# Two-layer hybrid denoiser: the first right operands made in two goes, and the last four readouts of a layer given places of their own and split where they stand

## The chip, the core and the metric

The kernel runs on one core of one Trainium2 chip. The core has TensorE (PE in the profile), which multiplies matrices from SBUF into PSUM; VectorE (DVE), ScalarE (ACT) and GpSimd (POOL), which work element by element; and SyncE (SP), which issues all of this kernel's DMA transfers, one behind the other. Each engine takes its instructions in a fixed order and waits on semaphores for what another engine, or a transfer, has to deliver first. The metric is the device time of one execution in microseconds; lower is better.

## The reference, cut to what matters

Two layers work on 512 latent columns and 256 context columns of width 1024. Each layer has a feed-forward block, a mixing stage and a second feed-forward block, and each of the three is fed with a normalised input that is scaled and shifted by values computed from a condition vector:

```
mx  = split(silu(c) @ w_mod[l] + b_mod[l], 9)        # shift, scale, gate of each of the 3 blocks
x  += 0.5 * mx[2] * swiglu(rms_norm(x)*(1+mx[1]) + mx[0], ffn_up, ffn_down)
...
p   = nx @ w_in[l]                                   # mixing
attn_x = neighbourhood_attention(q, k, v, ...)       # 4 head pairs
o   = o_fwd + o_bwd                                  # RWKV scans in both directions
o   = (o - mean(o)) * rsqrt(var(o) + eps) * lnx_gain + lnx_bias
rwkv_x = (o + bonus) * g                             # the readout
y_x = concat(attn_x, rwkv_x) @ w_out[l]              # the output projection
x  += mx[5] * y_x
```

The second feed-forward block has the form of the first. In the last layer the context is needed only as far as it feeds the latent part.

## The kernel before

All data are kept with features on the 128 partitions and the 768 columns (latent, then context) along the free axis. A product in near-float32 is made of three matmuls: each operand is split into a high part (ACT rounds it) and a low part (DVE subtracts the high part from the original), `split`, L208; lines L171 and L165 in the profile are the helpers that issue an ACT activation and an elementwise two-operand operation.

**Feed-forward blocks.** The up projection is a Strassen-Winograd product: features and columns are halved, and seven products replace eight. Its seven right operands are made from sums and differences of four quarters of the scaled input, and its left ones from those of the weights (`raw`; POOL makes s and rewrites raw). `prep_wino` (L258) makes the right operands of one of four feature tiles, with the tile four further on: it scales both (`xs0`, `xs1`) on ACT with the modulation's scale `gs`, appends two columns each of the modulation's shift (`mods[l][:, 3*s]`) for latent and context at the ends of the halves, so that the shift goes through the product as columns of its own, and makes seven high/low pairs (`part`; the tile name is `b`). Three differences are POOL's, one is DVE's. Each half has `XH` = 386 columns, of which the last four carry the shift. The root mean square is applied behind the product, so the operands do not need it. `prep_begin` (L216) asks for the first weights (`up_weights`) and hands out the places of the operands.

At the start `run` (L1119) makes modulation 1 (the scale; a layer has nine such, each from `mod`, L174: matmuls over weight tiles, here four of 2048 columns, a copy `modsb` on DVE, two transpositions, and the addition of the bias, `mods`, on DVE), loads x, makes modulation 0 (the shift) to its end, and then calls `prep_begin` and `prep_wino` four times. The first seven products of the up projection (PSUM tile `mw`, L369; their combination on DVE is `up_g<-up_g,mw`) follow.

**Mixing.** Six generators run at once: the RWKV chains, their solves, their blocks, the projections, the attention and the output projection, with the later modulations as another filler. `drive` (L81) gives them priorities, chains first; at the build a scheduler deals the instructions of each engine from these into one fixed order. RWKV's eight heads are two groups; a group's chain (`rwkv_chain`, L919) goes through six pieces of 128 tokens in both directions. When it has both directions of a piece, a readout follows (`rwkv_read`, L992): piece 0 and 1 are context, 3, 4, 2, 5 latent, and the chain's last two pieces release two readouts each, 3 and 4, then 2 and 5. A readout is

- `pj` (PE, the backward output turned over), `o` = forward + `pj` (DVE), mean and its subtraction (DVE, POOL, POOL), square (ACT), sum, root, reciprocal, product (DVE, ACT, DVE, POOL; the small results are `rst`);
- `pt` (two transpositions on PE), each scaled on ACT into `ry`; `ry` + `bv`, the bonus (POOL);
- `pg` (two matmuls on PE: the gate), `ry` times `pg` (DVE), and a store of both halves into `yd` in DRAM.

Its five SBUF tiles come from the pool `ro`, which has five places, thus one readout's worth; `pj`, `pt` and `pg` share the two PSUM banks of `a`. Other pools: `st`, eight places of 2048 columns; `x`, `r`, `g3`, `z`.

The output projection goes in four pairs of feature tiles: two of the attention (k = 0 to 3), that of RWKV's group 0 (k = 4, 5), and last that of group 1 (k = 6, 7). For each pair `mix_out` (L1032) loads both tiles from `yd` (`yl`, 128x768, or 128x512 in layer 1), splits them whole into `o2`, and runs 8 output tiles (`accumulate`, L428: `mm`, L327). Behind each output tile of the last pair `to_ffn` makes the operands of the second feed-forward block with `prep_wino`, whose first weights (`raw`) are asked for there.

Of the kernel before, what the change touches and what calls it, by code (L numbers as in the profile page):

```python
# [109 lines left out]
class Net:  # L110
# [147 lines left out]
    def prep_wino(self, kt, tag="g3"):  # L258

        l, s = self.prep_key  # L260
        h = self.half(self.prep_ctx)
        x0, x1 = [self.t(tag, f"xs{i}", 2 * XH) for i in range(2)]
        for k, t in ((kt, x0), (kt + 4, x1)):
            for xs, j in ((LAT, 0), (CTX, 1))[:2 if self.prep_ctx else 1]:
                self.act(t[:, xs], self.x[k][:, xs], AF.Copy, scale=self.gs[l, s][:, k, j:j + 1])
            self.act(t[:, 2 * h - 4:2 * h].rearrange("p (a c) -> p a c", a=2), free_ap(self.mods[l][:, 3 * s, k], [[0, 2], [1, 2]]), AF.Copy)
# [8 lines left out]
        part(1, x1[:, a])  # L275
        self.tt(x0[:, a], x0[:, b], x0[:, a], ALU.subtract, self.nc.gpsimd)
# [9 lines left out]
        self.squares(kt + 4)  # L286

# [631 lines left out]
    def rwkv_chain(self, l, i, last):  # L919
# [8 lines left out]
        for u in range(6):  # L928
            emit = not (last and u < 2)
            yield from self.until(lambda: g["applied"] > u)  # L930
            bl = lambda y, e, d, c: self.block(g["stage"][y, u], e, d, c)
# [28 lines left out]
            self.chained[i] = u + 1  # L960
            for b in ((), () if last else (0, 1), (), (), (3, 4), (2, 5))[u]:
# [29 lines left out]

    def rwkv_read(self, l, i, u, of, ob):  # L992
# [3 lines left out]
        bv = self.t("ro", "bv").rearrange("p (y t) -> p y t", y=2)  # L996
        for y in range(2):
            nc.sync.dma_start(out=bv[:, y], in_=self.bvd[2 * i + y][:, sl])
# [3 lines left out]
        o = self.t("ro", "o").rearrange("p (y e v) -> p y e v", y=2, e=2)  # L1002
# [6 lines left out]
        sq = self.t("ro", "osq").rearrange("p (n v) -> p n v", n=4)  # L1009
# [6 lines left out]
        yt = self.t("ro", "ry").rearrange("p (y t) -> p y t", y=2)  # L1016
# [4 lines left out]
        gg = self.t("ro", "gg")  # L1021
        nc.sync.dma_start(out=gg, in_=self.a["gg2"][l][:, 256 * i:256 * i + 256])
# [4 lines left out]
        n = NL + 128 * u if u < 2 else 128 * u - NC  # L1027
        for y in range(2):
# [3 lines left out]
    def mix_out(self, l, ctx, k0, n, tag, after):  # L1032
# [3 lines left out]
        for k in range(k0, k0 + n):  # L1036
            t = self.t("z", "yl", T)
            self.nc.sync.dma_start(out=t[:, 0:w], in_=self.yd[k][:, 0:w])
# [80 lines left out]
    def run(self, out):  # L1119
# [7 lines left out]
        for _ in self.mod(0, 0, "st", SW, "g"):  # L1127
            pass
# [132 lines left out]
```

## Time and profile before

| | us |
|---|---|
| median of 3 runs | 3911.8 (3909.35 to 3918.2) |
| profiled execution, its own time | 3917.2 |
| its span | 3915.4 |
| PE busy | 3616.3 (92%) |
| DVE busy | 2924.9 (75%) |
| ACT busy | 1496.0 (38%) |
| POOL busy | 1013.9 (26%) |

The profiled execution is 5.4 us above the median, and 1.8 us of it lie outside its span. The page divides the span into 40 slices of 97.9 us; a digit is the busy share of an engine in tenths, and the row PEclk is the clock granted to PE in tenths of full speed. A timeline row has the start in us from the span's start, the duration in us, the engine, the line, and the operation with its tiles, output first. SPq is a transfer that SP has issued. A view by stretch gives each engine's busy microseconds between two times, a view by lines groups equal instructions with their mean in ns.

### The profile page before, as it was taken

The numbers are of one execution on the slowest core, as the hardware profiler recorded it, in microseconds if no ns is written. First come the engines' busy times: TensorE is split into PE (matmuls) and PEld (weight loads), VectorE is DVE, ScalarE is ACT, GpSimd is POOL, SyncE is SP. The second block draws the span as 40 slices with busy tenths as digits, with TensorE's granted clock in tenths as the row PEclk, the third lists the DMA queues.
The fourth block names the chain that finished last, engine by engine and source line by source line (L and its number), as shares of the span: only waits on it lengthen the run. The fifth ranks groups of instructions, "written<-read, shape, count | busy, mean of one in ns | idle before, by whom it ended". The sixth has DMA issues, their size and how long they took to land. (4 is left out here: it accounts for less than half of the span.)

```text
span 3915.4 us, 73285 instructions
## 1 busy us (share of the span) xinstructions
PE 3616.3 (92%) x28980; PEld 3121.2 (80%) x28980; DVE 2924.9 (75%) x5618; ACT 1496.0 (38%) x2968; POOL 1013.9 (26%) x1156
## 2 busy tenths in 40 slices
PE   6999999999798898799999999999998996879999
PEld 4789998787565666699998999998786665768999
DVE  5678786666777765888788887886668677668988
ACT  4233334334343432533335333334434343234433
POOL 2222230202222211322224222230203223123443
PEclk7999999999797889899999999999998896788999
DMA  5421112322354243111121111113332431121222
GB/s 196 124 88 65 68 63 100 102 91 75 96 155 129 83 149 118 64 65 65 68 84 47 62 65 68 65 65 118 101 103 82 149 112 48 61 91 65 84 101 86
DMA packets 216535, 354.60 MB, mean 91 GB/s; under 512 B 46720, under 2 KB 131072, under 8 KB 203904
## 3 DMA queue, kind: packets, MB, share of 16 engines
q1 hardware_dynamic: 216192, 349.91, 27.4%
q8 instruction: 229, 3.75, 0.4%
q14 instruction: 114, 0.93, 0.1%
HBM read 306.31 MB, written 43.52 MB: 89 GB/s over the span
## 5 line engine op out<-in xcount | busy, mean ns | idle before, releaser
L369 PE MATMUL mw<-b,wq 128*128 128x386 f32 (+1 forms) x4224 | 787.0, 329 | 19.4 <-DVE wq L165 15.1
L369 PEld LDWEIGHTS mw<-b,wq 128*128 128x128 f32 x4224 | 704.0, 191 | 39.3 <-DVE wq L165 19.3
L327 PE MATMUL mm<-h,whi 128*128 128x256 f32 (+1 forms) x2816 | 652.6, 326 | 2.6 <-ACT h L171 0.8
L369 PE MATMUL mw<-b,whi 128*128 128x386 f32 (+1 forms) x2112 | 518.4, 328 | 24.6 <-DVE b L165 11.3
L327 PEld LDWEIGHTS mm<-h,whi 128*128 128x128 f32 x2816 | 467.6, 188 | 59.6 <-issue 8.5
L168 DVE SCALAR_TENSOR_TENSOR x<-mm,mods,x 128x256 f32<-128x256 f32 (+1 forms) x704 | 390.7, 581 | 159.5 <-PE mm L327 157.1
L327 PE MATMUL mm<-h,wlo 128*128 128x256 f32 (+1 forms) x1408 | 440.6, 325 | 2.7 <-DVE wlo L165 2.3
L369 PEld LDWEIGHTS mw<-b,whi 128*128 128x128 f32 x2112 | 374.1, 191 | 32.2 <-DVE b L165 14.0
L171 ACT ACTIVATE whi<-wraw 128x512 fp32r<-128x512 f32 x312 | 195.8, 629 | 500.2 <-PE mm L327 298.3
L165 DVE TENSOR_TENSOR wq<-raw,wq 128x512 fp32r<-128x512 f32 x352 | 313.2, 892 | 52.0 <-ACT wq L171 50.1
L369 PE MATMUL mw<-b,wlo 128*128 128x386 f32 (+1 forms) x1056 | 347.0, 329 | 3.4 <-DVE wlo L165 3.0
L171 ACT ACTIVATE wq<-raw 128x512 fp32r<-128x512 f32 x352 | 220.1, 629 | 312.1 <-PE mw L369 288.8
L327 PEld LDWEIGHTS mm<-h,wlo 128*128 128x128 f32 x1408 | 261.8, 188 | 29.5 <-DVE wlo L165 4.4
L165 DVE TENSOR_TENSOR wlo<-wraw,whi 128x512 fp32r<-128x512 f32 x312 | 224.9, 723 | 57.7 <-ACT whi L171 34.3
L165 DVE TENSOR_TENSOR up_g<-up_g,mw 128x386 f32<-128x386 f32 (+1 forms) x352 | 182.0, 518 | 86.1 <-PE mw L369 77.1
L165 POOL TENSOR_TENSOR raw<-raw,s 128x512 f32<-128x512 f32 x88 | 123.8, 1407 | 407.3 <-DVE wq L165 404.8
L165 POOL TENSOR_TENSOR s<-raw 128x512 f32<-128x512 f32 x88 | 125.2, 1423 | 394.8 <-DVE wlo L165 317.3
L171 ACT ACTIVATE whi<-s 128x512 fp32r<-128x512 f32 x176 | 110.0, 628 | 281.9 <-PE mm L327 198.9
L165 POOL TENSOR_TENSOR up_g<-up_g,rstd 128x386 f32<-128x386 f32 (+1 forms) x88 | 107.5, 1221 | 405.1 <-DVE up_g L165 405.1
L327 PE MATMUL mm<-x,whi 128*128 128x258 f32 (+2 forms) x832 | 208.5, 337 | 0.0
L369 PEld LDWEIGHTS mw<-b,wlo 128*128 128x128 f32 x1056 | 201.2, 191 | 7.4 <-DVE wlo L165 6.5
L188 PE MATMUL modps<-wmod,cs 128*32 128x256 f32 x1152 | 168.7, 441 | 30.7 <-DMA wmod<-in_w_mod_dram 30.0
(226 smaller groups left out, 7009.8 us busy)
## 6 DMA issues: line engine op xcount, KB each, us to landing
raw<-in_ffn_up_dram SPq DMA_DIRECT2D x88, 1024.0 KB, 5.2
wmod<-in_w_mod_dram SPq DMA_DIRECT2D x208, 256.0 KB, 3.0
wraw<-in_ffn_down_dram SPq DMA_DIRECT2D x176, 256.0 KB, 3.1
wraw<-in_w_in_dram SPq DMA_DIRECT2D x104, 256.0 KB, 2.8
wmod<-in_w_mod_dram SPq DMA_DIRECT2D x96, 128.0 KB, 2.3
wmod<-in_w_mod_dram SPq DMA_DIRECT2D x8, 1024.0 KB, 10.6
wraw<-in_w_out_dram SPq DMA_DIRECT2D x32, 256.0 KB, 3.2
in<-rkv SPq DMA_DIRECT2D x20, 384.0 KB, 4.2
```

What stands on the lines that cost most here:

```text
L165: (eng or self.nc.vector).tensor_tensor(out=out, in0=a, in1=b, op=op)
L168: self.nc.vector.scalar_tensor_tensor(out=out, in0=a, scalar=s, in1=b, op0=op0, op1=op1)
L171: self.nc.scalar.activation(out, in_, f, **kw)
L188: nc.tensor.matmul(ps[q:q + 32], lhsT=self.cs[:, kt], rhs=w, start=kt == 0, stop=kt == KD - 1)
L327: nc.tensor.matmul(ps, lhsT=wt, rhs=xt[k][:, c0:c1], start=k == 0 and n == 0, stop=k == nk - 1 and n == 2)
L369: nc.tensor.matmul(ps, lhsT=wt[:, c], rhs=self.bs[i][k][xt], start=k == 0 and m == 0, stop=k == 3 and m == 2)
```

## The change

**Right operands in two goes.** `run` now calls `prep_begin` ahead of modulation 0 and takes one step of that modulation behind each `prep_wino`. These four calls have `shifts=False`: operands 0 and 1 are made on all 386 columns, as before, but on what stands in the last four then; operands 2 to 6 on 382. What the last four columns will need of `xs0` and `xs1` POOL copies into a small tile `edge`. When the shift is there, `prep_shifts` makes the four differences of these columns for all tiles at once (DVE, 128x16) and splits them into the operands' last columns, 20 splits of 128x4.

**A layer's end.** In the last group (i = 1), when the chain comes to its fifth piece, four tiles of `st` are taken, one for each of the readouts 3, 4, 2 and 5 (name `read`, all five parts of a readout in it), and the bonus and the gate's weights are loaded into them at once (`read_begin`). Behind the fifth piece `last_inputs` takes two more, `o2`, the operands of the last pair; in layer 0 it fills their context columns from `yd`. The four readouts (`direct`) then split their product `yt` straight into the columns of `o2`, and `mix_out` takes `o2` for the last pair without a load. The diff, cut to its core:

```diff
@@ prep_wino @@
+            if shifts:
+                self.act(t[:, 2 * h - 4:2 * h]..., free_ap(self.mods[l][:, 3 * s, k], ...), AF.Copy)
...
-            self.split(src, hi, lo)
+            w = src.shape[-1]
+            self.split(src, hi[:, 0:w], lo[:, 0:w])
...
         part(1, x1[:, a])
+        if not shifts:
+            for i, t in enumerate((x0, x1)):
+                self.nc.gpsimd.tensor_copy(self.edge[:, i, kt], t[:, n:h])
+            a, b = slice(0, n), slice(h, h + n)
...
+    def prep_shifts(self):
...
+        self.tt(c[4], s0, e0, ALU.subtract)
+        self.tt(c[3], s1, s0, ALU.subtract)
+        self.tt(c[2], s1, c[4], ALU.subtract)
+        self.tt(c[6], c[2], e1, ALU.subtract)
+        c[5] = s1
+        for i in (2, 3, 4, 5, 6):
+            for k in range(4):
+                hi, lo = [t[:, n:h].rearrange("p (a c) -> p a c", a=2) for t in self.bs[i][k]]
+                self.split(c[i][:, k], hi, lo)
@@ rwkv_chain @@
+            if u == 4 and i == NG - 1:
+                self.reads = {n: self.read_begin(l, i, n, self.t("st", "read")) for n in (3, 4, 2, 5)}
...
+            if u == 4 and i == NG - 1:
+                self.last_inputs(last)
             for b in ((), () if last else (0, 1), (), (), (3, 4), (2, 5))[u]:
                 self.rwkv_read(l, i, b, obs[b], obs[(1 if b < 2 else 7) - b])
@@ last_inputs @@
+        self.o2 = [self.t("st", "o2", 2 * T, F32R).rearrange("p (a t) -> a p t", a=2) for _ in range(2)]
+        if not last:
+            for (hi, lo), k in zip(self.o2, range(2 * NP - 2, 2 * NP)):
+                t = self.t("z", "yl", T)
+                self.nc.sync.dma_start(out=t[:, CTX], in_=self.yd[k][:, CTX])
+                self.split(t[:, CTX], hi[:, CTX], lo[:, CTX])
@@ rwkv_read @@
+        direct = i == NG - 1 and u > 1
+        bv, gg, o, osq, ry = self.reads[u] if direct else self.read_begin(l, i, u)
...
+        if direct:
+            for y, (hi, lo) in enumerate(self.o2):
+                self.split(yt[:, y], hi[:, n:n + 128], lo[:, n:n + 128])
+            return
@@ mix_out @@
+        if k0 + n == 2 * NP:
+            hh, hl = zip(*self.o2)
+        else:
...
@@ run @@
-        for _ in self.mod(0, 0, "st", SW, "g"):
+        self.prep_begin(0, 0, True)
+        edge = self.t("ro", "edge", 96).rearrange("p (i k n) -> p i k n", k=4, n=4)
+        self.edge, self.ends = edge[:, 0:2], edge[:, 2:6]
+        steps = self.mod(0, 0, "st", SW, "g")
+        for k in range(4):
+            self.prep_wino(k, "x" if k < 3 else "g3", False)
+            next(steps, None)
+        for _ in steps:
             pass
-        self.prep_begin(0, 0, True)
-        for k in range(4):
-            self.prep_wino(k, "x" if k < 3 else "g3")
+        self.prep_shifts()
```

The build deals the start and both mixing stages anew; the feed-forward blocks stand as before, instruction by instruction. In the mixing stages operations of attention and modulation move by up to some 250 matmuls. PE issues as many matmuls as before (22154 with transpositions); DVE has 38 instructions more, ACT 28, POOL 8, and SP 18 transfers fewer.

**The start's order.** On DVE before, the addition that ends modulation 0 (`mods_76`; row 24 of this engine's order) has most splits `b` behind it, and so has the first addition of the up projection (`up_g`), which follows the last split:

```order
L299 RECIPROCAL rs<-sd 128x6
L190 COPY modsb<-modps 128x256
L165 TENSOR_TENSOR wlo<-s_387,whi 128x512
L165 TENSOR_TENSOR mods_76<-modpt,vecs_68 128x16
L165 TENSOR_TENSOR wlo<-s_386,whi 128x512
L165 TENSOR_TENSOR b<-xs_203,b 128x386
L165 TENSOR_TENSOR b<-xs_236,b 128x386
L165 TENSOR_TENSOR b<-xs_237,b 128x386
L165 TENSOR_TENSOR b<-xs_202,b 128x386 x2
```
...
```order
L165 TENSOR_TENSOR b<-xs_318,b 128x386
L165 TENSOR_TENSOR b<-xs_319,b 128x386 x2
L165 TENSOR_TENSOR xs_319<-xs_319 128x386
L165 TENSOR_TENSOR b<-xs_319,b 128x386
L165 TENSOR_TENSOR b<-xs_318,b 128x386 x2
L165 TENSOR_TENSOR b<-xs_319,b 128x386
L165 TENSOR_TENSOR up_g<-up_g,mw 128x386
L165 TENSOR_TENSOR wq<-raw,wq 128x512 x2
```

Now `mods_76` stands 23 rows later, behind 20 of the 28 large splits and two of weights (`wq`), and `up_g` stands ahead of the last large splits:

```order
L190 COPY modsb<-modps 128x256
L165 TENSOR_TENSOR b<-xs_243,b 128x382
L165 TENSOR_TENSOR wq<-raw,wq 128x512 x2
L165 TENSOR_TENSOR mods_76<-modpt,vecs_68 128x16
L165 TENSOR_TENSOR b<-xs_243,b 128x382
L165 TENSOR_TENSOR b<-xs_295,b 128x386
L165 TENSOR_TENSOR edge<-mods_76,edge 128x16
```
...
```order
L165 TENSOR_TENSOR edge<-edge 128x16
L165 TENSOR_TENSOR b<-edge,b 128x4 x7
L165 TENSOR_TENSOR up_g<-up_g,mw 128x386
L165 TENSOR_TENSOR wq<-raw,wq 128x512
L165 TENSOR_TENSOR xs_296<-xs_296 128x382
L165 TENSOR_TENSOR wq<-raw,wq 128x512
L165 TENSOR_TENSOR b<-xs_296,b 128x382
L165 TENSOR_TENSOR b<-xs_295,b 128x382
L165 TENSOR_TENSOR b<-edge,b 128x4
L165 TENSOR_TENSOR b<-xs_295,b 128x382
```

So 24 of the 28 large splits stand ahead of `up_g<-up_g,mw`, where all 28 did; the four differences and 17 of the 20 splits of four columns stand ahead of it too.

**PE at the end of layer 0's mixing.** `mm<-o` are matmuls of the output projection; the first is of its third pair (k = 4, 5), the last of its last pair. Before, three readouts stand between them, two of them whole:

```order
L327 MATMUL mm<-o_14611,wlo 128x256
L1018 MATMUL pt_15206<-consts,o 128x128
L1025 MATMUL pg<-sg,gg 128x128 x2
L1001 MATMUL pj<-ob,consts 128x256
L1018 MATMUL pt_15353<-consts,o 128x128 x2
L1025 MATMUL pg<-sg,gg 128x128 x2
L1001 MATMUL pj<-ob,consts 128x256
L1018 MATMUL pt_15385<-consts,o 128x128 x2
L1025 MATMUL pg<-sg,gg 128x128 x2
L327 MATMUL mm<-o_15402,whi 128x512
```

Now the third readout's `pj` stands further up, and these rows remain at the end:

```order
L352 MATMUL mm<-o_14657,whi 128x256
L352 MATMUL mm<-o_14656,wlo 128x256
L1067 MATMUL pt_15407<-consts,read 128x128
L1072 MATMUL pg<-sg,read 128x128 x2
L1067 MATMUL pt_15407<-consts,read 128x128
L1050 MATMUL pj<-ob,consts 128x256
L1067 MATMUL pt_15433<-consts,read 128x128
L1072 MATMUL pg<-sg,read 128x128 x2
L1067 MATMUL pt_15433<-consts,read 128x128
L352 MATMUL mm<-o_15218,whi 128x512
```

Between the third readout's `pj` and the first row shown stand 22 more rows of `mm` of the third pair, 24 in all. The fourth readout's `pj` has stayed behind the third's second transposition. In layer 1, where before rows of the third pair stood behind the chain's last product (`co`), none do now; they are done ahead of it.

**POOL at the end of layer 1's mixing.** `rst` and `o` (now `read`) belong to a readout's normalisation, `ry<-ry,bv` (now `read<-read`) adds the bonus, and `s<-raw`, `raw<-raw` are the first steps on the weights of the next feed-forward block. Before:

```order
L1007 TENSOR_SCALAR rst<-rst 128x4
L165 TENSOR_TENSOR o<-o,rst 128x256 x2
L165 TENSOR_TENSOR ry<-ry,bv 128x256
L1007 TENSOR_SCALAR rst<-rst 128x4
L165 TENSOR_TENSOR o<-o,rst 128x256 x2
L165 TENSOR_TENSOR ry<-ry,bv 128x256
L165 TENSOR_TENSOR s_34820<-raw 128x512
L165 TENSOR_TENSOR raw<-raw 128x512
```

Now:

```order
L1056 TENSOR_SCALAR rst<-rst 128x4
L165 TENSOR_TENSOR read<-read,rst 128x256 x2
L165 TENSOR_TENSOR s_34841<-raw 128x512
L165 TENSOR_TENSOR read<-read 128x256
L165 TENSOR_TENSOR raw<-raw 128x512
L1056 TENSOR_SCALAR rst<-rst 128x4
L165 TENSOR_TENSOR read<-read,rst 128x256 x2
L165 TENSOR_TENSOR read<-read 128x256
L1056 TENSOR_SCALAR rst<-rst 128x4
L165 TENSOR_TENSOR read<-read,rst 128x256 x2
L165 TENSOR_TENSOR read<-read 128x256
```

The two steps on the weights now stand ahead of the last two readouts' normalisation and, with `s<-raw`, ahead of an addition of the bonus. On SP the request for `raw` has moved up, several weight tiles of the output projection ahead of where it stood.

## Rows read from the trace of the kernel before

**Rows 1.** The page, part 2: busy tenths in 40 slices, and the clock.

```profile
PE   6999999999798898799999999999998996879999
...
DVE  5678786666777765888788887886668677668988
...
PEclk7999999999797889899999999999998896788999
```

**Rows 2.** Stretch: length, PE, PEld, DVE, ACT, POOL busy (count), clock, DMA share, GB/s.

```profile
27.27:44.05 16.78, 11.83 (x90) 7.45 (x82) 6.73 (x12) 9.26 (x16) 3.77 (x3) 0.61 0.64 245
44.05:73.57 29.52, 16.15 (x66) 10.88 (x67) 25.05 (x34) 15.22 (x40) 19.40 (x16) 0.65 0.22 72
640.00:1550.00 910.00, 829.66 (x8656) 627.07 (x8654) 609.91 (x1368) 345.01 (x747) 173.53 (x317) 0.89 0.36 111
```

**Rows 3.** Timeline of the start: start, us, engine, line, operation.

```profile
28.15 0.55 DVE L165 TENSOR_TENSOR b<-xs,b 128x386 fp32r<-128x386 f32 x1
...
38.62 1.93 PE L188 MATMUL modps<-wmod,cs 128*32 128x256 f32 x16
...
43.87 0.17 DVE L165 TENSOR_TENSOR mods<-modpt,vecs 128x16 f32<-128x16 f32 x1 [2.23 <-PE modpt L193]
...
44.08 0.78 ACT L171 ACTIVATE xs<-mods 128x4 f32<-128x4 f32 x7 [3.22 <-DVE mods L165]
...
71.59 1.98 DVE L165 TENSOR_TENSOR b<-xs,b 128x386 fp32r<-128x386 f32 x4
```

**Rows 4.** DVE splits and POOL subtractions by form: count, busy us, mean ns.

```profile
L165 DVE TENSOR_TENSOR b<-xs,b 128x386 fp32r<-128x386 f32 x7 | 8.8, 1313 | 0.4 <-ACT b L171 0.4
...
L165 POOL TENSOR_TENSOR xs<-xs,xs 128x386 f32<-128x386 f32 x8 | 8.9, 1111 | 0.5
```

**Rows 5.** Matmuls into mw by stretch, columns as in rows 2.

```profile
44.00:73.57 29.57, 13.46 (x46) 9.94 (x47) 0.09 (x1) 0.47 (x1) 0.65 0.22 72
73.57:83.55 9.98, 8.06 (x40) 6.44 (x38) 3.13 (x6) 0.00 (x0) 1.00 0.41 118
```

**Rows 6.** Timeline, end of layer 0's mixing.

```profile
1549.44 0.28 PE L327 MATMUL mm<-o,wlo 128*128 128x256 f32 x1
...
1550.72 0.70 PE L1001 MATMUL pj<-ob,consts 128*128 128x256 f32 x2
...
1555.80 0.33 PE L1018 MATMUL pt<-consts,o 128*128 128x128 f32 x1 [4.38 <-POOL o L165]
...
1557.81 1.12 PE L1001 MATMUL pj<-ob,consts 128*128 128x256 f32 x2
...
1565.91 0.42 DVE L165 TENSOR_TENSOR ry<-ry,pg 128x256 f32<-128x256 f32 x1 [3.63 <-POOL ry L165]
1566.36 0.79 SPq L1029 DMA_DIRECT2D y<-ry  x2
...
1571.79 0.79 PE L327 MATMUL mm<-o,whi 128*128 128x512 f32 x1 [6.35 <-ACT o L171]
```

**Rows 7.** Timeline, end of layer 1's mixing.

```profile
3472.71 0.28 PE L327 MATMUL mm<-o,wlo 128*128 128x256 f32 x1
...
3472.82 0.59 PE L1001 MATMUL pj<-ob,consts 128*128 128x256 f32 x2
...
3480.15 1.13 PE L1001 MATMUL pj<-ob,consts 128*128 128x256 f32 x2
...
3488.26 0.42 DVE L165 TENSOR_TENSOR ry<-ry,pg 128x256 f32<-128x256 f32 x1 [3.62 <-POOL ry L165]
...
3493.52 0.79 PE L327 MATMUL mm<-o,whi 128*128 128x256 f32 x2 [5.74 <-ACT o L171]
```

**Rows 8.** Timeline, load of next weights (layer 0) and last ob copy (layer 1).

```profile
1568.75 0.90 SPq L343 DMA_DIRECT2D raw<-in_ffn_up_dram  x2
...
1575.23 1.27 POOL L165 TENSOR_TENSOR s<-raw 128x512 f32<-128x512 f32 x1 [9.36 <-DMA raw<-in_ffn_up_dram]
...
3469.43 0.60 ACT L171 ACTIVATE ob<-co 128x512 f32<-128x512 f32 x1
```

More of the change, by code (lines that the diff above doesn't have):

```diff
@@ L265, in prep_wino @@
                 self.act(t[:, xs], self.x[k][:, xs], AF.Copy, scale=self.gs[l, s][:, k, j:j + 1])
-            self.act(t[:, 2 * h - 4:2 * h].rearrange("p (a c) -> p a c", a=2), free_ap(self.mods[l][:, 3 * s, k], [[0, 2], [1, 2]]), AF.Copy)
+            if shifts:
+                self.act(t[:, 2 * h - 4:2 * h].rearrange("p (a c) -> p a c", a=2), free_ap(self.mods[l][:, 3 * s, k], [[0, 2], [1, 2]]), AF.Copy)
         a, b = slice(0, h), slice(h, 2 * h)
@@ L286, in prep_wino @@
         self.squares(kt + 4)
+    def prep_shifts(self):
+        l, s = self.prep_key
+        h = self.half(self.prep_ctx)
+        n = h - 4
+        e0, e1 = [self.edge[:, i].rearrange("p k (a c) -> p k a c", a=2) for i in range(2)]
+        s0, s1 = [free_ap(self.mods[l][:, 3 * s, k], [[2, 4], [0, 2], [1, 2]]) for k in (0, 4)]
+        c = {i: self.ends[:, j].rearrange("p k (a c) -> p k a c", a=2) for j, i in enumerate((2, 3, 4, 6))}
+        self.tt(c[4], s0, e0, ALU.subtract)
[7 more added lines that the diff above has]
+                self.split(c[i][:, k], hi, lo)
     def prep_end(self):
@@ L990, in values_by_tokens, with last_inputs, read_begin @@
                     nc.sync.dma_start(out=dst, in_=t[QUADS[c], :, 64 * e:64 * e + 64])
+    def last_inputs(self, last):
+        self.o2 = [self.t("st", "o2", 2 * T, F32R).rearrange("p (a t) -> a p t", a=2) for _ in range(2)]
[4 more added lines that the diff above has]
+                self.split(t[:, CTX], hi[:, CTX], lo[:, CTX])
+    def read_begin(self, l, i, u, place=None):
+        sl = slice(128 * u, 128 * u + 128)
+        part = (lambda name, n: place[:, 256 * n:256 * n + 256]) if place is not None else (lambda name, n: self.t("ro", name))
+        ts = [part(name, n) for n, name in enumerate(("bv", "gg"))]
+        for y in range(2):
+            self.nc.sync.dma_start(out=ts[0][:, 128 * y:128 * y + 128], in_=self.bvd[2 * i + y][:, sl])
+        self.nc.sync.dma_start(out=ts[1], in_=self.a["gg2"][l][:, 256 * i:256 * i + 256])
+        return ts + [part(name, n + 2) for n, name in enumerate(("o", "osq", "ry"))]
     def rwkv_read(self, l, i, u, of, ob):
@@ L995, in rwkv_read @@
         sl = slice(128 * u, 128 * u + 128)
-        bv = self.t("ro", "bv").rearrange("p (y t) -> p y t", y=2)
-        for y in range(2):
-            nc.sync.dma_start(out=bv[:, y], in_=self.bvd[2 * i + y][:, sl])
+        direct = i == NG - 1 and u > 1
+        bv, gg, o, osq, ry = self.reads[u] if direct else self.read_begin(l, i, u)
+        bv = bv.rearrange("p (y t) -> p y t", y=2)
         pj = self.bank("a", "pj", (128, 2, 2, 64))
@@ L1093, in outs @@
                 self.reload()
-            yield from self.mix_out(l, not last, k, 2, "st" if i == 3 else "x", after if i == 3 else nop)
+            yield from self.mix_out(l, not last, k, 2, after if i == 3 else nop)
     def fillers(self, ids, tag, cols, bank, ready=lambda: True):
```

26 lines of the change are left out of this document (12 added, 14 removed).

## The prediction

> **What bounds the kernel now.** Read the page's second part first: PE is at 9 tenths or more in most of the 40 slices, and the first slice of the span, the seventeenth (from 1566 us) and the thirty-sixth (from 3426 us) are among the few low ones [rows 1]. So time can be won where PE waits; elsewhere PE sets the pace. Then the busy times by stretch: in the start, 27.27 to 73.57 us, DVE is busy 6.73 of 16.78 us and then 25.05 of 29.52; in the middle of layer 0's mixing PE is busy 829.66 of 910 us [rows 2]. Then the timeline at three places.
>
> At the start the shift of modulation reaches SBUF at 43.87; before it DVE made only three operand splits (one is shown), and the last is over at 73.57 [rows 3]. At the end of layer 0's mixing PE finishes the third quarter of the output projection at 1549.72 and starts the last at 1571.79; in layer 1 it is 3472.99 and 3493.52 [rows 6, 7]. These two gaps, 22.07 and 20.53 us, hold the last readouts one behind the other, and then the way through DRAM.
>
> **The change at the start.** It removes no large operation: the same 28 splits and 4 DVE subtractions, 20 of the splits on 382 columns instead of 386, then 20 splits and 4 subtractions of 4 or 16 columns, and 8 POOL copies of 4 columns. Scaling, splitting and subtracting no longer wait for 43.87. What can go is therefore DVE's idle time between 27.27 and 73.57: 16.78 - 6.73 + 29.52 - 25.05 = 14.5 us [rows 2]. Against it stand four costs.
> - The small DVE operations: 24 at between half and all of the 0.17 us of the 16-column addition [rows 3], 2.0 to 4.1, taken as 3.
> - ACT goes on making scaled copies and squares before it can give DVE more high parts; I take 4 us of DVE's idle time as staying, of some 10 ahead of 44 us.
> - POOL. A split is 0.55 us with POOL idle [rows 3], but 1.31 us on average (7 of them) while POOL subtracts at 1.11 [rows 4]. Before, POOL ran only 3.77 us ahead of 44 us; now its subtractions stand beside DVE's work from the first weights on. About four more DVE operations are stretched by 0.76: 3 us.
> - A new wait: DVE's first addition for the up projection (up_g<-up_g,mw) now stands ahead of the last four large splits [the start's order, in the section on the change], and it needs PE's second product, which needs the last feature tile's second part. Twelve matmuls at the half clock are 4 us, half of it hidden: 2 us.
> 14.5 - 3 - 4 - 3 - 2 = 2.5 us gained. The bounds: all the idle time goes and only the small operations stay, 12.5 won; or DVE and POOL get nothing done side by side, 3 lost (below). Because the estimate is near the lower end I keep 2.5. At 73.57 us, 46 of the first block's matmul records lay behind, 40 more follow by 83.55 [rows 5]; afterwards PE is the limit and the shift of the start is carried on.
>
> The Trainium skill, page "SBUF — State Buffer", section "SBUF: two separate sides", says that VectorE and GpSimd share one pair of SBUF ports under an exclusive lock: a VectorE operation with two SBUF inputs and a GpSimd operation wait for each other whole. The rows [rows 4] lean that way, 1.31 against 0.55, but the eight DVE operations between 46.2 and 56.3 took 10.1 us, in which POOL was also nearly always busy; by strict turns 8 x 0.55 and POOL's own 9 would be over 13. By the rule packing both engines closer wins nothing; by the rows it wins a part.
>
> **The change at a layer's end.** It removes, from each chain's end: the DRAM store of the readout, its load, and the splits of two whole tiles. In layer 0 that is from 1566.33 (end of the last multiply, 1565.91 + 0.42) to 1571.79: 5.5 us; in layer 1, 3488.68 to 3493.52: 4.8 us [rows 6, 7]. It adds splits of 128 columns: ACT does 128x128 in at most 0.46 (the two ry rows' kind, L171), so PE waits about 0.6 for the first high part. Net 4.9 and 4.2.
>
> It also gives each readout its own buffers. But pj, pt and pg, the three PSUM results, still rotate over two banks, and the new order on PE still has the fourth readout's pj behind the third's second transposition. One readout still follows another; from pj to pj is 7.33 us in layer 1 [rows 7]. What changes is how many stand behind the last projection matmul.
> - Layer 0: before, the third pj starts at 1550.72, 1 us behind that matmul. Now 24 matmuls come after it, at 2.5 us per twelve. A readout's pj to its first transposition is 5.08 us (1550.72 to 1555.80), so the third is ready about when the projection ends; I allow 1 us because DVE is busier then. From there to the fourth pj 2.0 (1555.80 to 1557.81), to the last multiply's end 8.5 (1557.81 to 1566.33), split 0.6: 12.1 instead of 22.07, 10 us gained [rows 6].
> - Layer 1: now no projection matmul is left behind the chain's last product, so the third pj starts 0.75 us behind it (ACT's copy of 0.60, [rows 8], and the hand-over); before, at 3472.82, it started just as the projection ended. So 0.75 + 7.33 + 8.53 + 0.5 = 17.1 instead of 20.53 [rows 7]: 3.5 us gained.
> A new wait hides here. POOL's first step on the next stage's weights (s<-raw, 1.27) now stands between a readout's normalisation and its last addition, the next one (raw<-raw) ahead of the following readout. Before, both stood behind all of them, and the weights came 6.5 us after their issue (1568.75 to 1575.23, [rows 8]). SP now issues that load several weight tiles earlier, so I take it as landed. If it isn't, POOL holds the readouts. Bounds: layer 0 from 2 to 12 won, layer 1 from 8 won to 1.5 lost.
>
> **Sum.** 2.5 + 10 + 3.5 = 16 us. The profiled execution took 3917.2 us (span 3915.4 and 1.8 around it), so it would take 3901.2; the runs' median, 3911.8, is 5.4 less, and the forecast is 3895.8. The build also deals the two mixing stages anew (attention and modulation work moves by up to some 250 matmuls); PE was idle 80 us of 910 there [rows 2], so a tenth of it, 8 us either way, belongs in the range.
>
> **The rivals.**
> - DVE and POOL take turns in full at the start, and the shift itself comes later: in the new order its addition (mods) stands 23 rows later on DVE. For: 1.31 against 0.55. Against: the overlap computed above. Start 3 lost: 3917.2 - 5.4 + 3 - 13.5 = 3901.
> - The last readouts run truly side by side: only one latency stands behind the projection. For: own buffers, earlier loads of bonus and gate. Against: the two PSUM banks and PE's order. Layer 0 then waits 5 us, layer 1 about 10: 17 and 10.5 won, 3911.8 - 30 = 3882.
> - The weights' load is late and POOL holds the readouts: two POOL steps of 1.27 in layer 0, about 5 us in layer 1. For: the order on POOL. Against: the earlier issue. 2.5 + 7.4 - 1.5 = 8.4 won: 3903.
> - Slower: the newly dealt mixing order costs PE. Its place is 640 to 1550 us and the same stage of layer 1; it decides once it takes more than the 16 won, a tenth of the 80 us of idle time in each layer; from 24 us in all the kernel is measurably slower. At 26 us: 3911.8 - 16 + 26 = 3922. For: PE waits for short chains there, so order matters. Against: the same work, limits and priorities; positions move a few per cent.
>
> **How the numbers follow.** Forecast 0.53 (its own range 3884 to 3907), turns 0.15, side by side 0.12, late weights 0.13, slower 0.07. A difference under 0.2%, 7.8 us, can't be told from none here, so faster means below 3904. Of the forecast 0.46 lies there, of turns 0.10, of side by side 0.12, of late weights 0.08: 0.76. Slower gets 0.06, the rest, 0.18, is no difference. Range 3874 to 3912: it takes in side by side and late weights, and leaves out the slower case and a start that wins all of its 12.5 on top.
>
> **What would show it.** Right: a gap on PE of about 12 us at layer 0's end and 17 at layer 1's, no store or load of y behind the last readouts, and DVE over 80% busy from 35 to 68 us, with splits of 1.2 us, the last large one near 68 to 71. Wrong at the start: operands complete by 62, or not before 74. Wrong at the ends: pj of the fourth readout not about 7 us behind the third's, or POOL's s<-raw waiting for DMA. Wrong altogether: PE's busy share in the mixing stages moved by over 1%.

## The result, and the profile after

The changed kernel takes 3878.9 us in the median of 4 runs (3867.5 to 3889.0) against 3915.0 for the kernel before (3909.4 to 3933.1): ratio 0.9899, 95% interval 0.9852 to 0.9947. It is faster, and by 36 us, where 16 were forecast. The time lies in the stated range (3874 to 3912), but that is luck in part: the range was drawn for other reasons than those that filled it. The profiled execution took 3871.0 us, 8 under this median, with a span of 3869.2, 46.2 less than before's.

The page's second part of the changed kernel, to be laid beside [rows 1]:

```profile
PE   6999999999899889899998999999999996879999
...
DVE  6578786666777675878888888886668777768988
...
PEclk8999999999798699899999999999999996789999
```

The lowest slices are where they were, the first, the thirty-fourth and the thirty-sixth; the eleventh and the seventeenth have a tenth more. No slice that was nearly empty has become full: the gain is spread. So the two traces are laid against each other by stages, each from one landmark on PE to the next (the last `mw` of a feed-forward block, the last `co` of a chain, the first `mm` behind the last `pg`, the first `mw`):

| stage | before, us | after, us | difference |
|---|---|---|---|
| start, to the end of the first feed-forward block | 585.8 | 579.7 | -6.1 |
| layer 0, mixing to the chain's last product | 935.4 | 934.4 | -1.0 |
| from there to the last pair's first matmul | 50.6 | 29.8 | -20.8 |
| last pair, to the next block's first `mw` | 32.4 | 30.8 | -1.7 |
| second and third feed-forward block | 1030.4 | 1031.7 | +1.4 |
| layer 1, mixing to the chain's last product | 834.8 | 827.0 | -7.8 |
| from there to the first `mm` behind the last `pg` | 24.1 | 17.6 | -6.5 |
| last pair, to the next `mw` | 25.7 | 21.4 | -4.4 |
| last block, to the end | 396.2 | 396.9 | +0.7 |

**The start.** Busy times by stretch of the changed kernel (columns as in [rows 2]: length, PE, PEld, DVE, ACT, POOL, clock, DMA share, GB/s), then two rows for `mw` alone as in [rows 5], which lack POOL:

```profile
27.27:44.05 16.78, 4.22 (x34) 1.57 (x34) 16.75 (x18) 12.16 (x24) 13.06 (x12) 0.50 0.74 303
44.05:68.98 24.93, 21.31 (x126) 16.10 (x127) 22.43 (x53) 13.54 (x43) 14.41 (x11) 0.82 0.17 50
```

```profile
44.00:68.98 24.98, 12.21 (x55) 10.42 (x56) 0.56 (x1) 0.47 (x1) 0.82 0.17 50
68.98:75.94 6.96, 6.05 (x34) 5.73 (x34) 2.66 (x5) 0.00 (x0) 1.00 0.36 109
```

DVE, idle for 10.05 of the first 16.78 us before, now works through them. The last large split ends at 68.99 instead of 73.57, and the reader sees in the timeline of DVE that the shift itself has come later, at 56.67 instead of 43.87 [rows 3], without holding anything up:

```profile
56.67 0.16 DVE L165 TENSOR_TENSOR mods<-modpt,vecs 128x16 f32<-128x16 f32 x1
...
60.55 1.18 DVE L165 TENSOR_TENSOR b<-mods,b 128x4 fp32r<-128x4 f32 x4
...
63.95 0.56 DVE L165 TENSOR_TENSOR up_g<-up_g,mw 128x386 f32<-128x386 f32 x1 [0.31 <-ACT up_g L171]
...
67.98 1.01 DVE L165 TENSOR_TENSOR b<-xs,b 128x382 fp32r<-128x382 f32 x2
```

**Layer 0's end.** The timeline of the changed kernel, to be read beside [rows 6]:

```profile
1526.80 0.60 PE L1050 MATMUL pj<-ob,consts 128*128 128x256 f32 x2
...
1531.89 0.28 PE L352 MATMUL mm<-o,wlo 128*128 128x256 f32 x1
...
1533.09 0.33 PE L1067 MATMUL pt<-consts,read 128*128 128x128 f32 x1 [0.92 <-POOL read L165]
...
1533.66 1.26 POOL L165 TENSOR_TENSOR s<-raw 128x512 f32<-128x512 f32 x1 [0.63 <-DVE wlo L165]
...
1534.85 0.70 PE L1050 MATMUL pj<-ob,consts 128*128 128x256 f32 x2 [0.55 <-ACT read L171]
...
1543.04 0.42 DVE L165 TENSOR_TENSOR read<-read,pg 128x256 f32<-128x256 f32 x1 [3.62 <-POOL read L165]
...
1543.86 1.22 PE L352 MATMUL mm<-o,whi 128*128 128x512 f32 x3 [2.15 <-ACT o L171]
```

The gap on PE reaches from 1532.17 to 1543.86: 11.7 us instead of 22.1. No store and no load of `y` stand in it (the one transfer issued there is a tile of the next block's weights, `raw`, at 1537.29), and the last multiply ends 0.4 us ahead of the first matmul. The third readout's `pj` runs beside the projection, its first `pt` is 0.9 us late, and the fourth readout's latency is what is left.

**Layer 1's end**, beside [rows 7]:

```profile
3432.38 0.97 PE L983 MATMUL co<-k,st 128*32 128x64 f32 x14
...
3434.39 0.70 PE L1050 MATMUL pj<-ob,consts 128*128 128x256 f32 x2 [0.78 <-ACT read L171]
...
3441.74 1.22 PE L1050 MATMUL pj<-ob,consts 128*128 128x256 f32 x2 [0.55 <-ACT read L171]
...
3443.34 0.92 PE L352 MATMUL mm<-o,whi 128*128 128x256 f32 x2 [0.38 <-ACT o L171]
...
3450.95 1.01 PE L352 MATMUL mm<-o,whi 128*128 128x256 f32 x3 [2.15 <-ACT o L171]
```

17.6 us from the chain's last product to the last pair's second column half; the first half's first output tile fits in between. From `pj` to `pj` it is 7.35, as before (7.33).

### The profile page after: what moved, and what is told of

Same layout as the page of the kernel before. It is cut to its first block, busy times and chain, and to the rows that moved or that the text cites. A ratio compares the mean times of both kernels' runs of the same rounds, so it can differ in the third digit from the quotient of the medians.

```text
span 3869.2 us, 73271 instructions
## 1 busy us (share of the span) xinstructions
PE 3598.2 (93%) x28980; PEld 3115.5 (81%) x28980; DVE 2937.1 (76%) x5656; ACT 1504.5 (39%) x2996; POOL 1014.1 (26%) x1164
```

## The experiments

Theory A: the gain is what the order of instructions fixes, at the start and behind the chain. Theory B: the luck of one execution. Theory C: the mixing stages have been dealt anew and that alone moves them. D and E are told where they come up. Each kernel was run 6 or 12 times beside the kernel before, 23 times, on the same chip; the ratios are to that one (medians of before 3916.8, 3916.5 and 3912.9 on the three chips). A difference between kernels of different chips, or one of single stages, comes from fewer numbers and is worth less. "Chain to last pair" is, as in the table above, the time from the end of a chain's last product (`co`) to the first `mm` behind the last `pg`; in layer 1 some matmuls of the last pair can come before that.

### The same kernel again, and each part alone

**again**: no edit.

> The changed kernel once more, with a profile of its own. Theory A (what the order of the instructions fixes): its 36 to 46 us against before come again stage by stage: start -6, the two mixing stages -11 each up to the last projection matmul ahead of the gap, gap of layer 0 about 12 us, from layer 1's last chain product to the last pair's second column group about 17.5. Theory B (a luck of one execution: clock and transfers): the mixing stages differ from the first profile by as much as they differ from before, 5 us or more per layer, and the time lies in the upper pair of its runs so far, 3887 to 3889.

Measured: 3875.1, ratio 0.9900 (0.9869 to 0.9931). Start 579.1, chain to last pair 29.9 and 17.6: as in the first profile, A holds there. But layer 0's mixing took 926.1 to the chain's end instead of 934.4. Nearly all of this arises in one place. Two rows, first of the changed kernel's first profile, then of the second, for `ap` (a blocks product) between 1255 and 1280 us; the three numbers are the shortest, the median and the longest in ns, then come the first and last start:

```profile
L789 PE MATMUL ap<-st,tt x96: 362/363/365, 1258.7 to 1273.2; 32*32 32x96 f32 x96
```

```profile
L789 PE MATMUL ap<-st,tt x96: 241/241/265, 1254.9 to 1264.2; 32*32 32x96 f32 x96
```

and the stretch 1250 to 1280 in the same two (the number behind POOL's is the granted clock):

```profile
1250.00:1280.00 30.00, 29.42 (x238) 20.89 (x236) 11.48 (x30) 10.32 (x24) 4.31 (x9) 0.53 0.17 48
```

```profile
1250.00:1280.00 30.00, 24.86 (x295) 18.43 (x293) 19.64 (x47) 18.69 (x38) 5.89 (x11) 0.84 0.15 47
```

The same instructions in the same order, 363 ns each in the one and 241 in the other: TensorE ran at 1.2 GHz there in the first execution and mostly at 2.4 in the second. Up to 1208 us the two executions agree within 0.6 us, from 1300 to the chain's end within 2.5 beside the 8 to 11 that were lost between. B is right in kind: two executions of one program can differ by some 8 us in a mixing stage, and here that is the clock. Why it fell in the one and not in the other is not shown.

**start_only**: the start's part of the diff (`prep_wino`, `prep_shifts`, `run`), the rest as before.

```diff
-        for _ in self.mod(0, 0, "st", SW, "g"):
+        self.prep_begin(0, 0, True)
...
+            self.prep_wino(k, "x" if k < 3 else "g3", False)
...
+        self.prep_shifts()
```

> Only the right operands in two goes; readouts and projection as before. Theory A: start -6; in layer 0 120 projection matmuls stand behind the chain's last product where 132 did, 12 fewer at 2.5 us per twelve, in layer 1 the same number, and both gaps stay at 22 and 20.5 us: in all -6 to -10 us. Theory C (the new dealing moves the mixing stage by chance, whatever is changed): a mixing stage moves by 5 us or more, of either sign, that the count of matmuls behind the chain does not explain.

Measured: 3916.8, ratio 0.9998 (0.9976 to 1.0020). The start gained 6.2 us, as in the pair. Both gaps stayed (49.9 and 24.3 from chain to last pair). But the mixing stages, in which nothing of the work was changed, took 5.4 and 3.2 us more in this profile, and by the median of 12 runs, too, the gain was gone: C.

**end_only**: the layer's end alone, the start as before; from its difference to the changed kernel:

```diff
+        for _ in self.mod(0, 0, "st", SW, "g"):
+            pass
...
-            self.prep_wino(k, "x" if k < 3 else "g3", False)
...
-        self.prep_shifts()
+            self.prep_wino(k, "x" if k < 3 else "g3")
```

> Only the layer's end; the start as before. Theory A: start 0. Layer 0: 36 matmuls (7.5 us) stand behind the chain's last product, then the rest of the second readout and two whole ones: 7.5 + 1 + 7.3 + 9 = 25 us from the chain's end to the last pair's first matmul, where before took 28.5 + 22.1 = 50.6: -25. Layer 1: 24 matmuls and the same readouts, 20.5 where before took 24.1: -3.5. In all about -29 us. If only the way through DRAM counts (theory D: the gain of a layer's end is the store, load and whole split of 5.5 and 4.8 us): -9.

Measured: 3898.3, ratio 0.9951 (0.9934 to 0.9968), -18.5 us, where A had -29 and D -9. From chain to last pair 26.3 in layer 0 (25 expected) and 20.8 in layer 1 (20.5): there A holds to about a microsecond. But layer 0's mixing took 15.5 us longer to the chain's end. Of the 132 projection matmuls that stood behind the chain's last product in the kernel before, 96 stand ahead of it here, 20 us of work. The stage's idle time on PE (79.2 us against 80.7) and its time at half clock (191 against 195) did not grow, so three quarters of the moved work seem to have come back there. That is read from one profile; no run moves the matmuls alone. Two whole readouts stand bare in this order:

```profile
1546.27 0.70 PE L1025 MATMUL pj<-ob,consts 128*128 128x256 f32 x2 [0.55 <-ACT read L171]
...
1552.29 0.47 PE L1042 MATMUL pt<-consts,read 128*128 128x128 f32 x1 [5.31 <-POOL read L165]
...
1554.38 1.22 PE L1025 MATMUL pj<-ob,consts 128*128 128x256 f32 x2 [0.55 <-ACT read L171]
...
1563.47 0.79 PE L327 MATMUL mm<-o,whi 128*128 128x512 f32 x1 [2.15 <-ACT o L171]
```

### The layer's end taken apart

**places_no_split**: places and early loads kept, store, load and whole split back.

```diff
...
-        if direct:
-            for y, (hi, lo) in enumerate(self.o2):
-                self.split(yt[:, y], hi[:, n:n + 128], lo[:, n:n + 128])
-            return
...
```

> The changed kernel with own places and early loads for the last four readouts, but their result stored to DRAM, loaded and split whole as before; the order on PE at both ends is nearly the changed kernel's. Theory A: from the last readout's multiply to the last pair's first matmul 5.5 us in layer 0 and 4.8 in layer 1, where the changed kernel takes 0.8 and 0.8, so 9 us slower than the changed kernel and no more; gap of layer 0 16 to 17 us. If the way through DRAM is hidden anyway: as fast as the changed kernel.

Measured: 3891.4, ratio 0.9939 (0.9915 to 0.9962), 16 us above the second timing of the changed kernel, where 9 and no more were expected. The timeline shows the price of the way through DRAM as expected, 5.6 us from the multiply's end to the first matmul, where the changed kernel has 0.4; layer 0's gap is 16.6:

```profile
1533.00 0.42 DVE L165 TENSOR_TENSOR read<-read,pg 128x256 f32<-128x256 f32 x1 [3.62 <-POOL read L165]
1533.45 0.80 SPq L1065 DMA_DIRECT2D y<-read  x2
1535.03 0.81 SPq L1074 DMA_DIRECT2D yl<-y  x2
...
1539.04 0.80 PE L352 MATMUL mm<-o,whi 128*128 128x512 f32 x1 [7.37 <-ACT o L171]
```

The way through DRAM is on the path. By stages the ends (chain to last pair) take 4.7 and 6.8 more than in the changed kernel's two profiles, the last pairs 2 and 3, layer 1's mixing 12, layer 0's 5 less. So the ends cost 11.5 where 9 were expected (in layer 1 24 matmuls stand behind the chain again), and the rest lies in the last pairs and in mixing stages dealt anew.

**split_no_places**: splits on the spot, tiles from `ro` when a readout begins.

```diff
-                self.reads = {n: self.read_begin(l, i, n, self.t("st", "read")) for n in (3, 4, 2, 5)}
...
-        bv, gg, o, osq, ry = self.reads[u] if direct else self.read_begin(l, i, u)
+        bv, gg, o, osq, ry = self.read_begin(l, i, u)
```

> The changed kernel with the splits on the spot, but the readouts' tiles from the pool ro again, one readout's worth, their loads asked for when a readout begins. Theory A (banks and order on PE hold the readouts, not the places): the gap of layer 0 is 12 to 13 us, from layer 1's chain end to the last pair 18 to 21 (24 matmuls stand behind the chain), the time within 8 us of the changed kernel's. Rival (the places are what helps): the readouts wait for a place and for their bonus, 2 us more each; gap of layer 0 over 15 us and at least 12 us slower than the changed kernel.

Measured: 3878.8, ratio 0.9907 (0.9885 to 0.9928): the same as the changed kernel. Gap of layer 0 11.5 us. In all, the places are worth nothing that can be measured here. Layer 1's end is longer, though, 22.4 from chain to last pair where the changed kernel takes 17.6 and 18 to 21 were expected: 24 matmuls stand behind the chain again, and the new wait that the prediction had named shows. POOL's second step on the next weights stands between a readout's mean (`rst`) and its subtraction and holds the readout by 1.3 us:

```profile
3440.02 0.22 POOL L1053 TENSOR_SCALAR rst<-rst 128x4 f32<-128x4 f32 x1 [0.56 <-DVE rst L1052]
3440.32 1.26 POOL L165 TENSOR_TENSOR raw<-raw 128x512 f32<-128x512 f32 x1
3441.54 0.61 POOL L165 TENSOR_TENSOR o<-o,rst 128x256 f32<-128x256 f32 x1
```

### The two PSUM banks

**banks_p**: the changed kernel, with

```diff
-        pt = self.bank("a", "pt2", (128, 2, 128))
+        pt = self.bank("p" if direct else "a", "pt2", (128, 2, 128))
...
-        pg = self.bank("a", "pg", (128, 2, 128))
+        pg = self.bank("p" if direct else "a", "pg", (128, 2, 128))
```

> The changed kernel, but the last readouts take their pt and pg from the two PSUM banks of p instead of a, which pj keeps. Theory A (two banks and the order on PE that follows from them hold one readout behind another): pj of the third and fourth readout stand together right behind the chain; in layer 0 72 matmuls (15 us) of the third pair stand behind the chain's last product, beside the readouts, and the last pair follows with a gap under 3 us: 16 from the chain's end where the changed kernel took 29.8, -14. Layer 1: 12.5 us where it took 17.6, -5. In all -19 against the changed kernel. Rival: the readouts' own operations on DVE, ACT and POOL hold them one behind another whatever the banks: the gap of layer 0 stays over 8 us, under -6 in all.

Measured: 3854.1, ratio 0.9838 (0.9806 to 0.9871): 21 us under the changed kernel on the same chip, 63 under before, and the fastest kernel here. Both `pj` stand together behind the chain, and in layer 0 PE goes on without a gap: 13.88 us from the chain's end to the last pair, 13.67 of them busy.

```profile
1507.53 1.02 PE L1050 MATMUL pj<-ob,consts 128*128 128x256 f32 x4
...
1519.33 0.28 PE L352 MATMUL mm<-o,wlo 128*128 128x256 f32 x1
1519.44 0.27 PE L1067 MATMUL pt<-consts,read 128*128 128x128 f32 x1
...
1519.92 0.71 PE L352 MATMUL mm<-o,whi 128*128 128x512 f32 x2
```

```profile
1506.04:1519.92 13.88, 13.67 (x82) 11.83 (x82) 11.14 (x28) 6.50 (x18) 4.65 (x8) 1.00 0.35 116
```

Layer 1 takes 12.7 (12.5 expected). So the banks, with the order on PE that follows from them, and not DVE, ACT or POOL, hold one readout behind the other in the changed kernel. Not all of it is kept: layer 0's last pair takes 34.1 us here and 30.8 in the changed kernel.

**banks_only**: the same two lines (for the last group's four readouts) in the kernel before.

```diff
+        pt = self.bank("p" if i == NG - 1 and u > 1 else "a", "pt2", (128, 2, 128))
...
+        pg = self.bank("p" if i == NG - 1 and u > 1 else "a", "pg", (128, 2, 128))
```

> The kernel before, with nothing changed but that the last four readouts of a layer take pt and pg from the PSUM banks of p. Theory A (the two banks hold one readout behind another): two pj stand together, the readouts run beside 60 matmuls of the third pair, and the gaps fall from 22 to about 10 us in layer 0 (the way through DRAM of 5.5 stays) and from 20.5 to 16 in layer 1: -15 us, with the dealing's +-10 on top. Rival (without places of their own the readouts still wait for the five tiles of ro): gaps within 3 us of before's.

Measured: 3917.6, ratio 1.0001 (0.9980 to 1.0022), no gain. Layer 0's gap is 14.6 us (1557.90 to 1572.53), so 7.4 less, not 12; chain to last pair 44.1 and 19.6, 11 us won together. The mixing stages gave 7.7 and 11.3 back. Here the places seem to matter: both `pj` stand together in layer 1, but there is one place for `o`, and DVE makes the second readout's `o` at 3489.78, when the first's second `pt` has read the first. So the second readout's `pt` comes 6 us behind the first's, where in banks_p it is 2.2 us (3428.09 and 3430.27). No run has the banks and the splits on the spot without the places, which would settle it.

```profile
3488.17 0.48 PE L1018 MATMUL pt<-consts,o 128*128 128x128 f32 x1 [3.67 <-POOL o L165]
...
3494.16 0.47 PE L1018 MATMUL pt<-consts,o 128*128 128x128 f32 x1 [3.63 <-POOL o L165]
```

### Dealt anew, work unchanged

**dealt_after**, **dealt_before**, **deal3_after**, **deal3_before**, **dealt_banks**: the chain's second number in the planner's table `E`, which `drive` reads, at 5.4 (deal3: 5.8); nothing else.

```diff
-E = dict(..., c=(0.1, 5.5), ...)
+E = dict(..., c=(0.1, 5.4), ...)
```

> The changed kernel with one number of the planner's table altered (the chain's second cost 5.4 in place of 5.5), so that the same instructions are dealt anew in the mixing stages; 84 projection matmuls stand behind layer 0's last chain product as in the changed kernel, none in layer 1. Theory C (how the mixing stages happen to be dealt is worth several us, whatever is changed): the time from the first feed-forward block's end to the chain's end differs by 5 us or more in a layer from the changed kernel's two profiles (934.4 and 926.1; 827.0 and 829.3), the total by 5 to 15 us. Theory E (the changed kernel's mixing is faster because of what it does): within 4 us of it, about 39 under before.

> The kernel before with the same number altered and nothing else. 120 projection matmuls stand behind layer 0's last chain product where 132 did, none in layer 1 where 24 did. Theory A alone (what no longer stands behind the chain is won): 2.5 + 3.4, so -6 against before. Theory C: the mixing stages move by 5 to 10 us each beside that, of either sign, and the kernel may win or lose up to 15 us without any change of its work.

> The changed kernel with the planner's number at 5.8, a third dealing of its mixing stages; about 900 rows of PE's order differ. Theory C: what the change is worth is the difference at the same number, free of a lucky dealing: 6 at the start, 13 at the two gaps, 5 in the projections behind them, 3 to 13 for matmuls that no longer stand behind the chain, so 27 to 37 under the kernel before at 5.8; against before at 5.5 anything from -10 to -45. Half-clock time in the mixing stages tells which, at 0.4 to 0.5 us each.

> The kernel before with the planner's number at 5.8; about 940 rows of PE's order differ, the rest is the same. Theory C: a mixing stage moves by 5 us or more from before's 935.4 and 834.8 (to the chain's end), with its half-clock time, at 0.4 to 0.5 us per us; total -10 to +15. Theory E (dealing is worth nothing): within 4 us of before.

> The version with pt and pg in the banks of p (63 us under before), its planner's number altered as in the other re-dealt kernels (5.4). Theory A and C: the ends keep what they won (14 us from layer 0's chain end to the last pair, 13 to 17 in layer 1), the mixing stages move: the total 5 to 20 us above it, still 10 to 19 under the re-dealt changed kernel. Theory E: as fast as it.

Measured, medians and ratios to before at 5.5 on the same chip; the stages are those of one profile each, with layer 0's and layer 1's mixing up to the chain's end and, in brackets, "half", the time at half clock in it (from the granted clock in stretches of 5 us, (1 - clock) x 2 x length):

| kernel | median | ratio (95%) | layer 0: mixing (half), chain to last pair | layer 1: the same |
|---|---|---|---|---|
| before, 5.5 | 3916.8 | | 935.4 (195), 50.6 | 834.8 (205), 24.1 |
| dealt_before, 5.4 | 3927.5 | 1.0025 (1.0001 to 1.0049) | 948.8 (236), 49.8 | 847.6 (212), 21.8 |
| deal3_before, 5.8 | 3926.8 | 1.0030 (1.0012 to 1.0047) | 927.2 (171), 50.7 | 838.1 (198), 23.7 |
| after, 5.5, two profiles | 3875.1 | 0.9900 (0.9869 to 0.9931) | 934.4 (198), 926.1 (177); 29.8, 29.9 | 827.0 (178), 829.2 (167); 17.6, 17.6 |
| dealt_after, 5.4 | 3895.5 | 0.9956 (0.9935 to 0.9977) | 944.8 (208), 29.7 | 839.2 (208), 17.6 |
| deal3_after, 5.8 | 3874.4 | 0.9907 (0.9879 to 0.9935) | 923.5 (174), 29.6 | 823.3 (188), 22.3 |
| dealt_banks, 5.4 | 3868.8 | 0.9887 (0.9868 to 0.9906) | 949.9 (222), 13.5 | 830.5 (198), 11.9 |

Theory E, that the mixing is faster because of what the change does and the dealing is worth nothing, falls: a number in a table moves the changed kernel by 20 us at 5.4 (by nothing at 5.8) and the kernel before by 11 and 14. Not all that two profiles differ by is the order, though. dealt_after and again keep within 1.5 us of each other from the first block's end to 1331 us. From 1332 the granted clock is 1.00 in again and stays at 0.50 in dealt_after, and at 1340 dealt_after is 7 us behind, while all records of PE still have the same names and shapes in the same order in both. The orders part at the record that starts at 1340.64 in again and at 1348.03 in dealt_after, and by 1440 us dealt_after is 18 us behind. The stretch 1327 to 1345 of again, then of dealt_after:

```profile
1327.00:1345.00 18.00, 18.00 (x267) 13.04 (x264) 9.47 (x23) 7.25 (x15) 1.56 (x3) 0.87 0.42 117
```

```profile
1327.00:1345.00 18.00, 18.00 (x161) 11.83 (x158) 5.22 (x11) 3.45 (x8) 0.72 (x1) 0.50 0.29 93
```

PE is busy throughout in both, with 267 matmuls at clock 0.87 and 161 at 0.50. So of these 18 us some 7 are the luck of an execution, as in again. The 20 us between the two kernels' medians stand on 12 runs of the one (3881 to 3914) and 6 of the other (3863 to 3888), and only the dealing differs between the two programs. At equal numbers the change is worth 41.7 us at 5.5, 32 at 5.4 and 52.4 at 5.8 (differences of the medians): 42 on average. For 5.8, 27 to 37 had been expected; and dealt_banks is 27 us under dealt_after, where 10 to 19 had been.

## Why the prediction was right in its mechanisms and too small in its sum

- **The two gaps**, 13.5 us forecast: right. Layer 0's gap fell by 10.4 (10 forecast), layer 1's by 2.9 against the 20.53 of [rows 7] (3.5 forecast). places_no_split shows the way through DRAM on the path (5.6 us), split_no_places that the places win nothing, banks_p that the two banks hold the readouts. In layer 0 of the changed kernel the third readout's `pj` starts 8.1 us ahead of the fourth's, in layer 1 7.35, one behind the other as forecast. The rival of readouts side by side was wrong for this kernel (gaps of 5 and 10 us) and right in kind for banks_p; that its time, 3882, is the nearest to the measured one is chance.
- **The new wait on POOL**: there, and small. In the traces `s<-raw` waited for no transfer; the two steps delayed nothing in the changed kernel by more than 0.4 us, and 1.3 in split_no_places. The late weights' rival is out.
- **The start**, 2.5 forecast, 6 to 7 measured in every kernel that has it at 5.5 (4.8 and 4.6 between the pairs at 5.4 and 5.8). Of 14.5 us of DVE's idle time 2.5 stayed, where I had taken 4; the wait for `up_g` was 0.3 us, not 2. DVE was busy 7.4 us longer (39.2 against 31.8), of which 4.1 lie in the small operations and 1.4 in two `wq` that now stand ahead; some 2 are left for stretching, for which I had 3. That makes 4.6 at the last split, and the rest lies in the products that PE had done by then, 55 records of `mw` against 46.

The rival with full turns was wrong in its time, 3 lost, but not because the two engines pass each other cheaply. On average splits took 0.87 and 0.90 us in this stretch, not the 1.31 of [rows 4], but these averages take in splits that met an idle POOL:

```profile
L165 DVE TENSOR_TENSOR b<-xs,b 128x382 fp32r<-128x382 f32 x16 | 13.6, 873 | 2.1 <-ACT b L171 2.1
L165 DVE TENSOR_TENSOR b<-xs,b 128x386 fp32r<-128x386 f32 x8 | 7.1, 903 | 0.0
```

Taken one by one, of the 28 large splits of the start 11 met an idle POOL and took 0.54 us each, and 11 with POOL busy for over nine tenths of their time took 1.05 on average and up to 1.63. Before, it was 13 at 0.55 and 8 at 1.25. Three rows of the timeline, where both engines are busy throughout:

```profile
30.66 1.59 POOL L165 TENSOR_TENSOR s<-s,raw 128x512 f32<-128x512 f32 x1
...
31.03 1.62 DVE L165 TENSOR_TENSOR b<-xs,b 128x382 fp32r<-128x382 f32 x1
...
32.20 1.59 POOL L165 TENSOR_TENSOR raw<-raw 128x512 f32<-128x512 f32 x1
```

There one split and one step of POOL's end every 1.55 us. Alone they take 0.54 and 1.26 (before, POOL at 37.07 with DVE idle), so whole turns would make it 1.80, an estimate from these two.

The Trainium skill, page "SBUF — State Buffer", section "SBUF: two separate sides", has an operation of VectorE with two SBUF inputs and one of GpSimd that reads SBUF shut each other out whole. These rows come near to that, 1.55 against 1.80. What the start won it won from DVE's idle time, and where POOL was not at work.

- **The term that was mis-sized** is the dealing. The prediction has it at nothing in the sum and writes "a tenth of it, 8 us either way, belongs in the range". I started to count at the gap and took the matmuls between the chain's last product and the gap as given. The order had them: 132 behind the chain's end in layer 0 before and 84 now, 24 and none in layer 1, 10 and 3.4 us at 2.5 us for twelve (1.7 for twelve of layer 1's, which are narrower). They left the end, and in the pairs the stage ahead of it did not get longer by as much: before against after at equal numbers, layer 0 from the first block's end to the last pair takes 22 to 30, 24 and 25 us less (5.5, 5.4, 5.8), layer 1 12 to 14, 13 and 16 (of single profiles, so with an execution's luck of some 8 us in each). Of these, some 25 in layer 0, the gap is 10.4. The last pairs add 3 to 6 us together, where I had nothing; in layer 1 one output tile of the pair, 1.7 us, now fits in the gap. So of the 36 us the start made 6 and the two gaps 13; the other 17 or so are this term and the last pairs.
- **Where that work went** is settled in part only. It does not seem to be hidden for free (end_only: 20 us moved, 15.5 longer). A fit to the 14 profiles makes layer 0's mixing out of a constant, its idle time, its time at half clock (0.45 us each) and the work moved ahead (0.7 of its time, but 0.5 when end_only is left out); it is typically off by 2.6 us, and by 6 in end_only. By it the changed kernel pays for half of the matmuls or more, and has less idle time (75.7 against 80.7) and, in its second profile, less time at half clock. That fit is an argument and no experiment. Why start and end together have this in three dealings of three, while the start alone loses 5 us in layer 0 and the end alone wins 9, stays open: the parts measure 0 and -18.5, together -41.7.
- "Faster" had a chance of 0.76 and came. The forecast's own range, 3884 to 3907, was too narrow by the spread of dealing, which runs now show as 10 to 20 us for one and the same work.

## What to carry to other kernels

When a change makes a scheduler deal a stage anew, count in the new order how many instructions of the bound engine stand behind the last link of the long chain, not only the wait behind them: that number was in the orders, and up to the last pair layer 0 won twice what its gap lost, though how much of that is theirs stays open. Judge a change of 1% on two or three dealings of the same work, since a planner's constant alone moved this kernel by 10 to 20 us. And ask which resource makes a serial tail serial before giving it buffers: here two PSUM banks did, and five SBUF tiles, by the trace of banks_only, once the banks were out of the way.

## What the runs showed of the hardware

Two executions of one program agreed within 0.6 us over more than 600 us of mixing and then parted by 10 us within 55, most of it in 30 us in which TensorE's granted clock was 0.53 in the one and 0.84 in the other. Ahead of that, from 1190 to 1210 us, PE had been busy for 16.3 and 17.3 of 20 us, at full clock in both; what decides in such a case is not shown. The executions of again and dealt_after parted the same way by 7 us, with the same records in the same order, at clock 1.00 and 0.50 from 1333 to 1340 us. A large DVE split took 0.54 us with POOL idle and 1.05 on average, single ones 1.63, with POOL busy beside it in the changed start, and 1.25 on average in the start before, so an average over a stretch is no price for the two engines side by side.
